# Second block of a two-block transformer: the meta tokens' value products as one product over 80 zero-padded rows

## The chip, the cores and the metric

The kernel runs on one core of a Trainium2 chip. The metric is the device time of one execution in microseconds (us). Of the kernel before, three runs are shown; their median is 2448.92 us (2448.57 to 2449.99).

## What is computed

Two transformer blocks follow each other on 512 tokens of width 1024, all in float32. The first block is a stick-breaking attention layer and a sparse attention layer, each with a squared-ReLU MLP. The change lies in the second block, which puts 16 meta tokens beside the 512 tokens and runs two attentions over all 528:

```python
u = rms_norm_2(h, g_mix)                       # h: meta tokens and the first block's output, 528 x 1024
qa, ka, va, qb, kb, vb, ga, gb = split(u @ w_in)
# diff_attention, 8 heads, two maps m per head, values 128 wide
p = softmax(q_m k_m^T / sqrt(64) - slope * dist)
w = p[0] - lam * p[1]
oa = rms_norm_2(w @ va, g_subln) * 0.8
# gqa_attention, 8 query heads, 2 key/value heads of 128
ob = softmax(axial_rope(qh) axial_rope(kh)^T / sqrt(128)) @ vb
merged = sigmoid(ga) * (oa @ w_branch_a) + sigmoid(gb) * (ob @ w_branch_b)
h = h + merged @ w_out
h = h + expert_choice_ffn(rms_norm_2(h, g_ffn))   # 16 experts, 66 tokens each
```

## The kernel before

Every float32 operand of a matrix product is kept in two float32r parts, h (the value rounded) and l (the rest), and a product x·w is made of three: h·h, l·h and h·l. Weights stream in as units of 128 x 1024: `unit` (L169) issues the load on SP's queue, ScalarE makes w_h (L185) and GpSimd or VectorE makes w_l (L186). `proj2` (L797) multiplies a unit with all 528 tokens in two halves of 264 columns; its products have the line L208.

The token axis is cut into five tiles, `TT`: four of 128 tokens and, last, the 16 meta tokens. Keys are taken in these five tiles, queries in two halves, `QH`: tiles 0 and 1 (256 queries), then tiles 2, 3 and the meta tile (272 queries).

Values: `vproj2` (L836) takes, for each token tile, 24 products (three kinds times 8 slices of 128 inputs) with the tile's columns of uh or ul as the stationary operand and 256 columns of the weights moving; the meta tile has a stationary operand of 16 columns. ScalarE writes the h part of the result, scaled by the token's factor rt, and VectorE the l part (L846, L847). `vproj2u` (L813) does the same for the first pair of heads, with all five tiles in three PSUM banks, so that the products don't wait for rt (L824, L830, L831). There are five such projections: four pairs of heads of the differential attention, and one for the grouped-query attention.

Attention: per head and query tile, the scores go into PSUM (L998 to L1003, and L1133), VectorE and ScalarE make the softmax (L1004 to L1012, L1135 to L1139), and the weights stay as row tiles e (queries on the partitions, 528 keys along). `av2` (L849) turns them and multiplies them with the values. For each key tile k it transposes each query tile's block on TensorE (L862), with as many rows and columns as the tiles have; ScalarE copies the result as h part pt_h (L866), VectorE makes pt_l (L867), and three products vh·pt_h, vl·pt_h and vh·pt_l are summed in the bank `av` (L871). For the meta tile of keys these three have a contraction of 16 rows. For the meta tile of queries the transposes have 16 rows:

```python
nc.tensor.transpose(pt[0:kn, c:c + qn], w[t][0:qn, ko:ko + kn], self.ident[0:qn, 0:qn])
```

So `av2` runs 32 times (8 heads, two halves, two attentions), with 25 transposes per head, five of them from the meta tile of queries.

A scheduler puts the instructions of all engines in an order, from the order in the code, the operands and the pools' buffers; each engine then runs its own list in that order. While a head's softmax runs, TensorE's list holds projections of later heads. The pools that the change touches: e0 (6 buffers of 128 x 528), e1 (3), v (2), the PSUM pools `tr` (2 banks), `av` (1), `mm` and `sc`. After the two attentions follow the gates and output projections (`merge`) and the experts, whose weights are most of the data that the kernel reads.

Of the kernel before, what the change touches and what calls it, by code (L numbers as in the profile page):

```python
# [7 lines left out]
F32 = mybir.dt.float32  # L8
F32R = mybir.dt.float32r
# [12 lines left out]
def ounits(w, groups):  # L22
    """Output weights by group of head pairs, in units of some columns for all pairs of the group."""
# [114 lines left out]
class Kern:  # L138
# [83 lines left out]
    def square(self, kt, eng=None, pool=False):  # L222
        """acc += x^2"""
# [20 lines left out]
    def rs(self, eps, rt, rr, pp=None):  # L244
        """rt[128, 4]: 1/rms by token on the partitions; rr[128, 512]: the same along the free axis."""
# [49 lines left out]
    def vproj(self, xh, xl, src):  # L295
        """x times two weight units; the four token tiles lie in two banks, each with one start for both of its tiles."""
# [27 lines left out]
    def av_causal(self, P, off, v, po, first, last):  # L324
        """po += v.T @ P.T for a causal P kept as row tiles at the offsets off."""
# [110 lines left out]
    def oproj(self, src, groups, todo, os_, after):  # L436
        """Output projection of the units todo of (group, unit), added to the residual."""
# [33 lines left out]
    def rope_sum(self, src, f, pool, pp, on_pool=0):  # L471
        """src * cos + rot(src) * sin, where f has the two parts of src."""
# [56 lines left out]
    def cmp_in(self, kp, c, xs, pos):  # L529
        """The compression blocks with their positions added, by block position pair and block, in two parts."""  # L530
# [12 lines left out]
    def cmp_raws(self, kp, k0):  # L543
        """Compression weights from unit k0 on, loaded ahead into the place of tiles that are done with."""
# [268 lines left out]
    def vproj2u(self, src, rt, v):  # L813
        """vproj2 with all token tiles at once, two in a bank, so that the products need no wait for rt"""
# [3 lines left out]
        for u in range(2):  # L818
            w = self.unit(src[u])
            for t, (o, n) in enumerate(self.TT):  # L820
                p = ps[t // 2][0:n, t % 2 * 256:t % 2 * 256 + 256]
                for a, (x, wi) in enumerate(((self.uh, 0), (self.ul, 0), (self.uh, 1))):
                    for k in range(4):
                        nc.tensor.matmul(p, x[:, u * 4 + k, o:o + n], w[wi][:, k * 256:k * 256 + 256],  # L824
                                         start=u == 0 and t % 2 == 0 and a == 0 and k == 0,
                                         stop=u == 1 and (t % 2 == 1 or t == 4) and a == 2 and k == 3)
        for t, (o, n) in enumerate(self.TT):
            p = ps[t // 2][0:n, t % 2 * 256:t % 2 * 256 + 256]
            r = rt[0:n, t:t + 1]
            nc.scalar.activation(v[0:n, t, 0], p, AF.Copy, scale=r)  # L830
            nc.vector.scalar_tensor_tensor(v[0:n, t, 1], p, r, v[0:n, t, 0].bitcast(F32), op0=OP.mult, op1=OP.subtract)  # L831
# [4 lines left out]
    def vproj2(self, src, rt, v):  # L836
        nc = self.nc
        wv = [self.unit(src[i]) for i in range(2)]
        for t, (o, n) in enumerate(self.TT):
            ps = self.mm.tile([128, 512], F32, name="mm")[0:n, :256]  # L840
# [801 lines left out]
```

## Time and profile before

| | before |
|---|---|
| median of three runs | 2448.92 us |
| the profiled execution: span from its first instruction to its last | 2447.4 us |
| TensorE products busy | 2357.8 us, 96% |
| VectorE busy | 1561.4 us, 64% |
| ScalarE busy | 1264.1 us, 52% |
| GpSimd busy | 677.3 us, 28% |
| share of the chain that ended last, by engine | PE 55%, DVE 6%, issue 4%, DMA 3%, POOL 2%, ACT 2% |

For the profiled execution the span is the only time on record; its time by the clock of the runs isn't shown, so the span is set against the median: 1.5 us less.

How to read it: PE is TensorE's products, PEld its loads of stationary operands, DVE VectorE, ACT ScalarE, POOL GpSimd. Where a form such as 16*128 stands with a product, it is the stationary operand: 16 rows (the contraction) by 128 columns (the rows of the result). A group's mean is the length of one instruction from its start to its modelled end; products overlap, so the steps between starts, not these lengths, add up to the stretch.

### The profile page before, as it was taken

What the parts mean: (1) busy time and instruction counts of PE and PEld (TensorE: products, weight loads), DVE (VectorE), ACT (ScalarE), POOL (GpSimd) and SP (SyncE); (2) the same over time, 40 slices, a digit from 0 to 9 for tenths busy, and PEclk for the clock granted to TensorE, in tenths of its full rate; (3) what the DMA queues carried; (4) which work ended last, traced back from release to release, by engine and by line L of the source; (5) the groups of instructions that cost most, each with busy time, mean ns of one, the idle gap of its engine ahead of it and who ended that gap; (6) DMA issues with size and microseconds to landing.
All of it is one profiled execution on the core that took longest, in us unless ns stands there. A gap on an engine that the chain in (4) does not pass through costs nothing.

```text
span 2447.4 us, 36010 instructions
## 1 busy us (share of the span) xinstructions
PE 2357.8 (96%) x13626; PEld 1946.2 (80%) x13626; DVE 1561.4 (64%) x2754; ACT 1264.1 (52%) x2269; POOL 677.3 (28%) x573
## 2 busy tenths in 40 slices
PE   8999999999989999899999999999999999699997
PEld 7887788888877777688888899889899999566664
DVE  6887543444586878643443677867666654588996
ACT  6665423223355767523223456555465533378885
POOL 0000322223325444222222632333454311111100
PEclk9999999999999999999999999999999999899998
DMA  4222223222432111122222321222211144689994
GB/s 143 78 78 87 69 95 95 95 95 95 132 120 77 36 37 43 52 95 95 94 90 93 123 79 53 70 60 63 70 44 44 44 174 155 229 302 370 375 390 144
DMA packets 85806, 286.57 MB, mean 117 GB/s; under 512 B 12197, under 2 KB 14117, under 8 KB 85633
## 3 DMA queue, kind: packets, MB, share of 16 engines
q1 hardware_dynamic: 79008, 273.78, 33.4%
q0 software_dynamic: 3360, 8.12, 1.6%
q10 hardware_dynamic: 3264, 2.38, 0.4%
q8 instruction: 107, 1.75, 0.3%
q14 instruction: 67, 0.54, 0.1%
HBM read 257.05 MB, written 12.37 MB: 110 GB/s over the span
## 4 chain that ended last, share of the span: by engine, by line
PE 55%; DVE 6%; issue 4%; DMA 3%; POOL 2%; ACT 2%; POOLq 0%; DVEq 0%; SPq 0%; ACTq 0%
PE mm L208 28%; PE mm L1495 5%; PE av L871 3%; PE mm L843 2%; PE mm L1517 2%; PE tr L862 2%; PE av L346 2%; PE mm L1048 1%; PE sc L1133 1%; PE mm L450 1%; PE tr L336 1%; PE sc L998 1%; PE sc L741 1%; PE sc L1003 1%; DMA res<-in_e_gate_dram 1%
## 5 line engine op out<-in xcount | busy, mean ns | idle before, releaser
L185 ACT CAST w_h<-w_raw 128x1024 fp32r<-128x1024 f32 x269 | 281.3, 1046 | 374.5 <-PE mm L208 285.9
L186 DVE TENSOR_TENSOR w_l<-w_raw,w_h 128x1024 fp32r<-128x1024 f32 x209 | 316.4, 1514 | 235.1 <-ACT w_h L185 234.4
L208 PE MATMUL mm<-uh,w_h 128*128 128x512 f32 (+1 forms) x1440 | 315.2, 352 | 14.6 <-ACT w_h L185 8.7
L208 PE MATMUL mm<-uh,w_l 128*128 128x512 f32 (+1 forms) x1440 | 309.0, 348 | 0.0
L208 PE MATMUL mm<-ul,w_h 128*128 128x512 f32 (+1 forms) x1440 | 306.1, 346 | 0.0
L208 PEld LDWEIGHTS mm<-uh,w_h 128*128 128x128 f32 x1440 | 238.5, 191 | 53.7 <-ACT w_h L185 9.0
L208 PEld LDWEIGHTS mm<-uh,w_l 128*128 128x128 f32 x1440 | 237.3, 190 | 35.9 <-issue 0.6
L208 PEld LDWEIGHTS mm<-ul,w_h 128*128 128x128 f32 x1440 | 234.9, 188 | 34.2
L186 POOL TENSOR_TENSOR w_l<-w_raw,w_h 128x1024 fp32r<-128x1024 f32 x60 | 144.8, 2417 | 158.2 <-ACT w_h L185 156.5
L782 POOL TENSOR_TENSOR relu<-relu 128x512 f32<-128x512 f32 x64 | 98.4, 1537 | 271.9 <-ACT hh L781 265.5
L780 ACT ACTIVATE relu<-mm 128x512 f32<-128x512 f32 x64 | 38.3, 598 | 232.6 <-PE mm L208 232.6
L788 POOL TENSOR_TENSOR res<-res,mt 128x512 f32<-128x512 f32 x62 | 90.4, 1459 | 214.1 <-DVE mt L787 214.1
L787 DVE TENSOR_TENSOR mt<-mm,rs 128x512 f32<-128x512 f32 x64 | 44.1, 690 | 139.0 <-PE mm L208 139.0
L208 PE MATMUL mm<-hh,w_h 128*128 128x512 f32 x512 | 131.4, 397 | 0.0
L208 PE MATMUL mm<-hh,w_l 128*128 128x512 f32 x512 | 130.7, 395 | 0.0
L208 PE MATMUL mm<-hl,w_h 128*128 128x512 f32 x512 | 130.7, 395 | 0.0
L235 POOL TENSOR_TENSOR acc<-acc,sq 128x512 f32<-128x512 f32 x28 | 42.5, 1519 | 304.9 <-ACT sq L233 304.6
L1495 PE MATMUL mm<-ul,xe 128*66 128x512 f32 x412 | 119.2, 397 | 0.1
L208 PEld LDWEIGHTS mm<-hh,w_h 128*128 128x128 f32 x512 | 95.9, 189 | 25.2 <-ACT w_h L185 3.4
L208 PEld LDWEIGHTS mm<-hh,w_l 128*128 128x128 f32 x512 | 96.6, 189 | 22.4
L208 PEld LDWEIGHTS mm<-hl,w_h 128*128 128x128 f32 x512 | 96.6, 189 | 22.4
L186 DVE TENSOR_TENSOR ol<-w_raw,ul 128x1024 fp32r<-128x1024 f32 x86 | 103.3, 1221 | 15.2 <-ACT ul L185 11.6
(525 smaller groups left out, 5439.6 us busy)
## 6 DMA issues: line engine op xcount, KB each, us to landing
w_raw<-in_w_dram SPq DMA_DIRECT2D x128, 512.0 KB, 3.5
w_raw<-in_e_down_dram SPq DMA_DIRECT2D x37, 512.0 KB, 11.1
w_raw<-in_e_gate_dram SPq DMA_DIRECT2D x34, 512.0 KB, 10.6
w_raw<-in_e_up_dram SPq DMA_DIRECT2D x34, 512.0 KB, 12.1
raws<-in_e_gate_dram SPq DMA_DIRECT2D x20, 512.0 KB, 11.0
raws<-in_e_up_dram SPq DMA_DIRECT2D x20, 512.0 KB, 11.4
raws<-in_e_down_dram SPq DMA_DIRECT2D x19, 512.0 KB, 11.7
res<-in_e_gate_dram SPq DMA_DIRECT2D x10, 512.0 KB, 10.6
```

Source lines behind the costliest of these rows:

```text
L185: nc.scalar.copy(h, raw)
L186: (nc.gpsimd if self.we else nc.vector).tensor_tensor(l, raw, h.bitcast(F32), op=OP.subtract)
L208: nc.tensor.matmul(ps, w[:, k * 128:(k + 1) * 128], x[k], start=start and a == 0 and k == 0, stop=stop and a == 2 and k == nk - 1)
L346: nc.tensor.matmul(po[:, j * 128:512], v[j], src[:, c:c + w], start=first and j == 0 and s == 0, stop=last and gi == 2 and s == 1)
L782: nc.gpsimd.tensor_tensor(r, r, r, op=OP.mult)
L787: nc.vector.tensor_tensor(t, ps, r2, op=OP.mult)
L788: (nc.vector if c == 3 and m == 7 else nc.gpsimd).tensor_tensor(res[:, m, 0:512], res[:, m, 0:512], t, op=OP.add)
L843: nc.tensor.matmul(ps, x[:, k, o:o + n], wv[k // 4][wi][:, (k % 4) * 256:(k % 4 + 1) * 256], start=a == 0 and k == 0, stop=a == 2 and k == 7)
L862: nc.tensor.transpose(pt[0:kn, c:c + qn], w[t][0:qn, ko:ko + kn], self.ident[0:qn, 0:qn])
L871: nc.tensor.matmul(po, x(k), y[0:kn, c], start=k == 0 and a == 0, stop=k == 4 and a == 2)
L1495: nc.tensor.matmul(ps, x[:, 2 * i + k], w[:, k * 512:k * 512 + 512], start=i == 0 and a == 0 and k == 0, stop=i == 3 and a == 2 and k == 1)
L1517: self.pe_last = nc.tensor.matmul(py[j], x[:, k], w[:, j * 512:j * 512 + 512], start=k == 0 and a == 0, stop=k == 3 and a == 2)
```

## The change

In the second block alone:

- The values of the meta tile go into a tile of their own, v4 (96 x 256, zeroed once): h part in rows 0 to 15, l part in rows 32 to 47, h part again in rows 64 to 79. The turned weights of the meta keys go into p4 (zeroed, two of them in turn): h part in rows 0 to 15 and 32 to 47, l part in rows 64 to 79. One product over rows 0 to 79 then sums the three (`av2`).
- The weights of the meta queries are kept in e4 (128 x 528, two in turn, zeroed), of which only the first 16 rows are written; every transpose takes 128 rows and the whole identity, so those of the meta queries have 128 moving columns in place of 16.
- In the V projections the meta tile's columns of uh and ul lie side by side in um (128 x 8 x 48, zeroed, uh in columns 0 to 15, ul in 32 to 47). One product with w_h gives both, in rows 0 to 15 and 32 to 47 of PSUM; `vkeep` adds the two with a copy on ScalarE and an addition on VectorE. 16 products per projection take the place of 24.
- The pool e0 has 5 buffers in place of 6, the value tiles 4 token tiles in place of 5; the zeroing is done by GpSimd.

The rest of the diff is comments, and `rank` and others are unchanged. Its core:

```diff
-    def vproj2u(self, src, rt, v):
+    def vproj2u(self, src, rt, v, v4):
...
+    def vmul(self, p, w, u, t, start, stop):
+        nc = self.nc
+        o, n = self.TT[t]
+        xs = ((self.uh, 0), (self.ul, 0), (self.uh, 1)) if t < 4 else ((self.um, 0), (self.uh, 1))[::1 - 2 * u]
+        for a, (x, wi) in enumerate(xs):
+            for k in range(4):
+                y = x[:, u * 4 + k] if x is self.um else x[:, u * 4 + k, o:o + n]
+                nc.tensor.matmul(p[0:y.shape[-1]], y, w[wi][:, k * 256:k * 256 + 256], start=start and a == 0 and k == 0,
+                                 stop=stop and a == len(xs) - 1 and k == 3)
+
+    def vkeep(self, p, rt, v, v4, t):
+        nc = self.nc
+        r = rt[0:self.TT[t][1], t:t + 1]
+        if t < 4:
+            h, l = v[:, t, 0], v[:, t, 1]
+        else:
+            h, l = v4[0:16], v4[32:48]
+            m = self.tp.tile([128, 512], F32, name="sq", bufs=2)[0:16, 0:256]
+            nc.scalar.copy(m, p[32:48])
+            nc.vector.tensor_tensor(m, p[0:16], m, op=OP.add)
+            p = m
+            nc.scalar.activation(v4[64:80], p, AF.Copy, scale=r)
+        nc.scalar.activation(h, p, AF.Copy, scale=r)
+        nc.vector.scalar_tensor_tensor(l, p, r, h.bitcast(F32), op0=OP.mult, op1=OP.subtract)
...
+    def meta_tiles(self, at):
+        nc = self.nc
+        e, p = ([at.tile([128, n], F32 if a == "e4" else F32R, name=f"{a}{i}") for i in range(2)] for a, n in (("e4", 528), ("p4", 272)))
+        for x in e + p:
+            nc.gpsimd.memset(x if x.dtype == F32 else x.bitcast(F32), 0.0)
+        self.e4, self.p4 = itertools.cycle(e), itertools.cycle(p)
...
-            kn = self.TT[g[0]][1]
             for j, k in enumerate(g):
-                ko = self.TT[k][0]
+                ko, kn = self.TT[k]
                 for t in tiles:
-                    qo, qn = self.TT[t]
-                    c = j * on + qo - o0
-                    nc.tensor.transpose(pt[0:kn, c:c + qn], w[t][0:qn, ko:ko + kn], self.ident[0:qn, 0:qn])
+                    c = j * on + self.TT[t][0] - o0
+                    nc.tensor.transpose(pt[0:kn, c:c + 128], w[t][:, ko:ko + kn], self.ident)
             n = len(g) * on
+            if g[0] == 4:
+                h = next(self.p4)[:, :n]
+                for o in (0, 32):
+                    nc.scalar.copy(h[o:o + 16], pt[0:16, :n])
+                nc.vector.tensor_tensor(h[64:80], pt[0:16, :n], h[0:16].bitcast(F32), op=OP.subtract)
+                nc.tensor.matmul(po, v4[0:80], h[0:80], start=False, stop=True)
+                continue
...
+                    full = at.tile([128, 528], F32, name="e0", bufs=5) if t < 4 else next(self.e4)
...
+                    self.vb4 = kp.tile([96, 256], F32R, name="vb4")
+                    nc.gpsimd.memset(self.vb4.bitcast(F32), 0.0)
+                    self.um = kp.tile([128, 8, 48], F32R, name="um")
+                    nc.gpsimd.memset(self.um.bitcast(F32), 0.0)
+                    nc.scalar.copy(self.um[:, :, 0:16], self.uh[:, :, 512:528].bitcast(F32))
+                    nc.scalar.copy(self.um[:, :, 32:48], self.ul[:, :, 512:528].bitcast(F32))
```

The scheduler makes new lists from this. TensorE's list in the grouped-query attention, in the first half of a head's queries. vb is the tile of values, e a tile of softmax weights, k and q keys and queries; a row's shape is that of the result. Before:

```order
L1133 MATMUL sc<-k_16006,q 128x264 x6
L208 MATMUL mm<-ul,w_h 128x264 x4
L871 MATMUL av<-pt_h,vb 128x256 x2
L208 MATMUL mm<-ul,w_h 128x264 x2
L871 MATMUL av<-pt_l,vb 128x256
L862 MATMUL tr<-ident,e_16504 128x128
L862 MATMUL tr<-ident,e_16530 128x16
L862 MATMUL tr<-ident,e_16517 128x128
L862 MATMUL tr<-ident,e_16530 128x16
```

With the change, at the same place:

```order
L1169 MATMUL sc<-k_15948,q 128x264 x6
L208 MATMUL mm<-ul,w_h 128x264 x7
L208 MATMUL mm<-uh,w_h 128x264 x3
L884 MATMUL tr<-ident,e_16274 128x128
L891 MATMUL av<-p_16276,vb_11546 128x256
L884 MATMUL tr<-ident,e_16451 128x128
L884 MATMUL tr<-ident,e_16464 128x128
L884 MATMUL tr<-ident,e_16274 128x128
```

The three L871 rows over the 16 meta keys (two from pt_h, one from pt_l, with projections in between) have become the one L891, which stands 10 rather than 4 projection products behind the scores; the meta queries' transposes (e_16530, now e_16274) write 128 columns in place of 16.

TensorE's list where the last V projection (of the grouped-query attention) ends. um is the tile with both parts of the meta tokens' x. Before:

```order
L843 MATMUL mm<-w_l,uh 128x256 x8
L881 MATMUL tr<-sq,ones 128x272
L843 MATMUL mm<-w_h,uh 16x256 x8
L843 MATMUL mm<-w_h,ul 16x256 x8
L843 MATMUL mm<-w_l,uh 16x256 x8
```

With the change:

```order
L834 MATMUL mm<-w_l,uh 128x256 x4
L891 MATMUL av<-p_11578,v_11584 128x272
L834 MATMUL mm<-w_h,um 48x256 x4
L834 MATMUL mm<-w_l,uh 16x256 x8
L834 MATMUL mm<-w_h,um 48x256 x4
```

24 products for the meta tile have become 16, eight of them with a stationary operand of 48 columns.

GpSimd's list where the differential attention starts. w_l is the l part of a weight unit; acc is the sum of squares of the first block's output. Before:

```order
L186 TENSOR_TENSOR w_l<-w_raw,w_h 128x1024
L235 TENSOR_TENSOR acc<-acc,sq 128x512
L186 TENSOR_TENSOR w_l<-w_raw,w_h 128x1024 x5
L1011 TENSOR_SCALAR e_11867<-e_11867,st,lam 128x528
```

With the change:

```order
L235 TENSOR_TENSOR acc<-acc,sq 128x512
L870 MEMSET e_11575 128x528
L870 MEMSET e_11576 128x528
L870 MEMSET p_11577 128x272
L870 MEMSET p_11578 128x272
L993 MEMSET v_11583 96x256
L993 MEMSET v_11584 96x256
L186 TENSOR_TENSOR w_l<-w_raw,w_h 128x1024 x5
```

Six fills stand ahead of the third weight unit's l part; the first two units and acc are ahead of them, as before.

## Rows read from the trace of the kernel before

**Rows 1.** Busy time by stretch: differential attention, grouped-query attention, experts.

```profile
core 0: us, PE busy (x) PEld busy (x) DVE busy (x) ACT busy (x) POOL busy (x), PEclk, DMA share, GB/s
1425.00:1725.00 300.00, 295.76 (x2278) 273.90 (x2277) 224.98 (x690) 173.97 (x397) 92.42 (x65) 1.00 0.20 59
1765.00:1960.00 195.00, 195.00 (x1489) 178.98 (x1488) 123.66 (x319) 117.37 (x271) 85.14 (x77) 1.00 0.14 44
2143.00:2400.00 257.00, 256.93 (x1232) 156.52 (x1232) 227.78 (x235) 213.68 (x260) 35.34 (x24) 0.99 0.98 357
```

**Rows 2.** What PE waited for, 1425 to 1725 us (total, times, longest).

```profile
PE av L871 <- DVE pt_l L867: 2.0, 1, 2.0
```

**Rows 3.** Timeline of PEld, first meta-key products (start, length, then the form).

```profile
1446.09 0.66 PEld L843 LDWEIGHTS mm<-w_h,uh 128*128 128x128 f32 x5
1446.89 0.29 PEld L871 LDWEIGHTS av<-pt_h,v 16*128 16x128 f32 x2
1447.32 0.30 PEld L843 LDWEIGHTS mm<-w_h,uh 128*128 128x128 f32 x2
...
1447.77 0.31 PEld L843 LDWEIGHTS mm<-w_h,ul 128*128 128x128 f32 x2
1448.21 0.18 PEld L871 LDWEIGHTS av<-pt_l,v 16*128 16x128 f32 x1
1448.53 0.20 PEld L862 LDWEIGHTS tr<-ident,e 128*128 128x128 f32 x2
```

**Rows 4.** Timeline of PEld, one of the last meta-key products.

```profile
1961.16 0.91 PEld L208 LDWEIGHTS mm<-uh,w_h 128*128 128x128 f32 x7
1962.21 0.29 PEld L871 LDWEIGHTS av<-pt_h,vb 16*128 16x128 f32 x2
1962.63 0.19 PEld L208 LDWEIGHTS mm<-uh,w_h 128*128 128x128 f32 x1
```

**Rows 5.** Timeline of PEld, a transpose of the meta queries.

```profile
1456.63 0.26 PEld L862 LDWEIGHTS tr<-ident,e 128*128 128x128 f32 x2
1457.05 0.14 PEld L862 LDWEIGHTS tr<-ident,e 16*128 16x128 f32 x1 [0.17 <-issue]
1457.22 0.19 PEld L998 LDWEIGHTS sc<-ks,qd 128*128 128x128 f32 x1
```

**Rows 6.** PE's groups by form (count | busy us, mean ns | idle before).

```profile
L862 PE MATMUL tr<-ident,e 16*128 16x16 f32 x64 | 13.0, 225 | 0.0
L871 PE MATMUL av<-pt_h,v 16*128 16x272 f32 x16 | 4.1, 336 | 0.0
L871 PE MATMUL av<-pt_l,v 16*128 16x272 f32 x8 | 3.1, 386 | 0.0
L862 PE MATMUL tr<-ident,e 16*16 16x16 f32 x16 | 2.9, 178 | 0.0
```

**Rows 7.** Timeline of PEld, a stationary operand of 16 columns behind one of 128.

```profile
1538.22 0.19 PEld L1003 LDWEIGHTS sc<-ks,qd 128*128 128x128 f32 x1
1538.33 0.10 PEld L998 LDWEIGHTS sc<-ks,qd 128*16 128x16 f32 x1
```

**Rows 8.** Timeline of PEld in the experts: a transpose over 66 rows.

```profile
2163.41 0.37 PEld L1495 LDWEIGHTS mm<-ul,xe 128*66 128x66 f32 x2
2163.88 0.14 PEld L1482 LDWEIGHTS tr<-ident,ya 66*128 66x128 f32 x1
2164.11 0.20 PEld L1495 LDWEIGHTS mm<-ol,xe 128*66 128x66 f32 x2
```

**Rows 9.** What DVE waited for, 1425 to 1725 us.

```profile
DVE st L1008 <- ACT e L1007: 17.8, 31, 1.8
DVE e L1004 <- PE sc L1003: 17.0, 24, 3.2
```

**Rows 10.** Groups by form of ACT, DVE and POOL, 1400 to 1980 us.

```profile
L866 ACT CAST pt_h<-tr 16x272 fp32r<-16x272 f32 x16 | 5.9, 370 | 12.4 <-PE tr L862 12.4
L867 DVE TENSOR_TENSOR pt_l<-tr,pt_h 16x272 fp32r<-16x272 f32 x16 | 6.8, 426 | 10.1 <-ACT pt_h L866 10.0
L1011 POOL TENSOR_SCALAR e<-e,st,lam 128x528 f32<-128x528 f32 x32 | 25.7, 804 | 100.9 <-DVE st L1008 85.0 <-DVE st L1006 8.5 <-PE tr L862 3.8
```

**Rows 11.** Timelines where the differential attention starts: POOL, then ACT.

```profile
1389.52 1.28 POOL L235 TENSOR_TENSOR acc<-acc,sq 128x512 f32<-128x512 f32 x1 [1.97 <-ACT sq L233]
1398.27 2.39 POOL L186 TENSOR_TENSOR w_l<-w_raw,w_h 128x1024 fp32r<-128x1024 f32 x1 [7.47 <-ACT w_h L185]
...
1389.90 0.28 ACT L908 CAST uh<-mt 128x128 fp32r<-128x128 f32 x1
1391.59 0.31 ACT L911 ACTIVATE mt<-res 128x128 f32<-128x128 f32 x1 [1.41 <-DVE ul L909]
```

More of the change, by code (lines that the diff above doesn't have):

```diff
@@ L819, in vproj2u @@
             w = self.unit(src[u])
[L820 to L831, printed above, removed]
+            for t in range(5):
+                self.vmul(ps[t // 2][:, t % 2 * 256:t % 2 * 256 + 256], w, u, t, u == 0 and t % 2 == 0, u == 1 and (t % 2 == 1 or t == 4))
@@ new lines, in vproj2u @@
+        for t in range(5):
+            self.vkeep(ps[t // 2][:, t % 2 * 256:t % 2 * 256 + 256], rt, v, v4, t)
+    def vmul(self, p, w, u, t, start, stop):
[7 more added lines that the diff above has]
+                                 stop=stop and a == len(xs) - 1 and k == 3)
@@ L833 @@
     VB = ("mm", "tr", "tr")
     VH = (0,)
-    def vproj2(self, src, rt, v):
-        nc = self.nc
-        wv = [self.unit(src[i]) for i in range(2)]
-        for t, (o, n) in enumerate(self.TT):
-            ps = self.mm.tile([128, 512], F32, name="mm")[0:n, :256]
-            for a, (x, wi) in enumerate(((self.uh, 0), (self.ul, 0), (self.uh, 1))):
-                for k in range(8):
-                    nc.tensor.matmul(ps, x[:, k, o:o + n], wv[k // 4][wi][:, (k % 4) * 256:(k % 4 + 1) * 256],
-                                     start=a == 0 and k == 0, stop=a == 2 and k == 7)
-            r = rt[0:n, t:t + 1]
-            nc.scalar.activation(v[0:n, t, 0], ps, AF.Copy, scale=r)
-            nc.vector.scalar_tensor_tensor(v[0:n, t, 1], ps, r, v[0:n, t, 0].bitcast(F32), op0=OP.mult, op1=OP.subtract)
@@ L849, in av2, with vproj2 @@
-    def av2(self, at, w, half, vh, vl):
+    def vproj2(self, src, rt, v, v4):
+        wv = [self.unit(src[i]) for i in range(2)]
+        for t in range(5):
+            ps = self.mm.tile([128, 512], F32, name="mm")[:, :256]
+            for u in range(2):
+                self.vmul(ps, wv[u], u, t, u == 0, u == 1)
+            self.vkeep(ps, rt, v, v4, t)
+    def meta_tiles(self, at):
+        nc = self.nc
+        e, p = ([at.tile([128, n], F32 if a == "e4" else F32R, name=f"{a}{i}") for i in range(2)] for a, n in (("e4", 528), ("p4", 272)))
+        for x in e + p:
+            nc.gpsimd.memset(x if x.dtype == F32 else x.bitcast(F32), 0.0)
+        self.e4, self.p4 = itertools.cycle(e), itertools.cycle(p)
@@ L851, in av2 @@
+    def av2(self, at, w, half, vh, vl, v4):
         nc = self.nc
@@ L870, in av2 @@
                 for a, (x, y) in enumerate(((vh, h), (vl, h), (vh, l))):
-                    nc.tensor.matmul(po, x(k), y[0:kn, c], start=k == 0 and a == 0, stop=k == 4 and a == 2)
+                    nc.tensor.matmul(po, x(k), y[:, c], start=k == 0 and a == 0, stop=False)
         return po
@@ L960, in diff_attention @@
         os_, late = [], []
+        self.meta_tiles(at)
+        v4s = [at.tile([96, 256], F32R, name=f"v4{i}") for i in range(2)]
+        for x in v4s:
+            nc.gpsimd.memset(x.bitcast(F32), 0.0)
         for head in range(8):
             if head % 2 == 0:
[L963 to L964 removed]
+                v = at.tile([128, 4, 2, 256], F32R, name="v", bufs=2)
+                v4 = v4s[head // 2 % 2]
+                (self.vproj2u if head in self.VH else self.vproj2)(I["a_v"][head:head + 2], self.rt, v, v4)
             sl = at.tile([128, 128], F32R, name="sl", bufs=2)
```

26 lines of the change are left out of this document (13 added, 13 removed).

## The prediction

> **What bounds the kernel now.** I read the busy time by stretch first. In the differential attention TensorE is busy 295.76 of 300 us, in the grouped-query attention all of 195 [rows 1]; VectorE, the next, has 75% and 63%. TensorE's own list of waits in the first stretch has as its longest entry one of 2.0 us, a product behind pt_l [rows 2]. So in both attentions time is the sum of TensorE's steps, and what shortens a step shortens the run, until another engine takes over. Behind them the experts run 257 us with the DMA engines at 98% [rows 1]; their loads start when buffers of the attentions and of the merge come free, so they move up with the attentions.
>
> Then I looked at what a step costs, in the timeline of the loads of stationary operands (PEld). Loads come one per product. Five of them with 128 rows stretch over 0.66 us [rows 3]; one is 0.19 long [rows 4], so the step is (0.66 − 0.19)/4 = 0.12 us. Where the 16-row products of the meta keys come in, it is longer. The last of those five starts at 1446.09 + 0.66 − 0.19 = 1446.56; two 16-row loads follow at 1446.89 and the next 128-row load at 1447.32 [rows 3]. That is 0.76 us for three steps, which should take 0.36: **0.40 us too much**. The single 16-row load behind it shows the same: from 1447.89 (1447.77 + 0.31 − 0.19) to 1448.53 is 0.64 for two steps, 0.40 too much. Near the end of the grouped-query attention it is 0.75 for three steps, 0.39 too much [rows 4]. So the engine pays for going to 16 rows and for coming back, about 0.2 us each way, whatever the number of products between.
>
> **What the change removes.**
>
> *Meta-key products.* `av2` runs 32 times. Each time two 16-row products from pt_h and one from pt_l become one: 64 products of 0.12 us, 7.7 us. In the trace the pair and the single product lie apart, with projections between [rows 3], so each run of `av2` pays two visits: 64 × 0.40 = 25.6 us, if 80 rows cost no visit. Together 33.3 us.
>
> *Transposes of the meta queries.* 64 with a 16*128 operand and 16 with 16*16 [rows 6]. A single one: the 128-row transposes ahead of it start last at 1456.63 + 0.26 − 0.14 = 1456.75, and the load behind it comes at 1457.22 [rows 5]: 0.47 us for two steps, 0.23 too much. With 128 rows and 128 columns it costs one common step, as its neighbours do (0.26 − 0.14 = 0.12 us from one to the next, [rows 5]). Some of the 80 stand side by side and share a visit. Always alone gives 80 × 0.23 = 18.4 us, always in pairs 9.2 us; I take 60 visits, 13.8 us, since the list of TensorE puts 128-row transposes between most of them.
>
> *V projections.* Five, each with 24 − 16 = 8 products fewer: 40 × 0.12 = 4.8 us. The stationary operand grows from 16 to 48 columns. A load of 16 columns behind one of 128 comes 0.11 us later [rows 7], no more than a common step, so a narrow operand costs no visit today, and I take none for 48 columns. The Trainium skill speaks against this: TensorEngine Tiling (Array Packing), section Key Properties, says that a change of tiling mode drains the engine, and lists 32, 64 and 128 columns as different modes. By that, 48 and 16 columns side by side would need a change in each of the ten units, and at 0.4 us each the sum would be 4 us smaller; the row above shows no such drain for columns.
>
> The sum of what TensorE is spared: 33.3 + 13.8 + 4.8 = **51.9 us**, of which some 28 in the differential attention (half of the first two, all of the third) and 24 in the other.
>
> **What it adds.**
>
> *80 rows instead of 16.* The trace of before has no product with 80 rows. The nearest is a transpose with 66 in the experts: the loads around it stand at 2163.64 (2163.41 + 0.37 − 0.14), 2163.88 and 2164.11, the pace of the 512-column products next to it (2163.41 to 2163.64), and the second load behind it follows after 0.20 − 0.14 = 0.06 us, the short step of a 66-column transpose [rows 8]. So it costs no visit. Ends: nothing, or 32 × 0.40 = 12.8 us as with 16 rows. I take nothing, as 80 is nearer to 66.
>
> *ScalarE.* One more copy into p4 per run of `av2`, 32 × 0.37 = 11.8 us; two more operations per V projection at about the same price, 3.7 us. They lie beside TensorE's products, since ScalarE is busy 174 of 300 and 117 of 195 us [rows 1, 10]. The chain from the transposes to the meta product grows by the copy, 0.37 + 0.37 + 0.43 in place of 0.37 + 0.43 for the l part; the scheduler's new list has ten projection products ahead of it where four stood, 1.2 us. If that cover is missing, the chain is the stall of the rival below.
>
> *VectorE.* Five additions of about 0.43 us: 2 us in 495.
>
> *GpSimd.* Fills: six at the start of the differential attention, four at that of the other, two earlier. None is in the trace; from below nothing, from above a tensor-scalar operation over 128 x 528, 0.80 us [rows 10], though four of the six are half as wide. Six are under 4.8 us and stand where GpSimd now waits 7.47 us for the next unit's h part [rows 11]. I take nothing. Without that gap the third unit's l part would come later, and the projection behind it.
>
> *The opening.* The first copy into um stands between L908 and L911 on ScalarE, the second behind L911, about 0.28 us each [rows 11]; the sums of squares for rt wait for L911. Also, the first copy lets the meta products of the first V projection start later. I take 1 us, ends 0 and 2.
>
> *New waits.* With 28 us less, VectorE's 225 us would fill 83% of 272. It already waits for ScalarE and for the scores, 17.8 and 17.0 us [rows 9], so it isn't evenly loaded, and in places it will hold TensorE. Ends: nothing, or half of the gain there, 14 us. I take 5 us, nearer the first, because TensorE today waits for it almost never [rows 2].
>
> **The forecast.** 51.9 − 1 − 5 = 46 us. Against the profiled span, 2447.4 − 46 = 2401.4 us; the median of the runs is 1.5 us higher, 2448.9 − 46 = **2403 us**.
>
> **The rivals.**
>
> 1. *VectorE becomes the bound in the differential attention.* For: its share, and ScalarE's chain through it. Against: the grouped-query attention, with 63%, has no such limit. The gain there is halved and the forecast's 5 us become 14: 2412 us; with waits in the other attention as well, 2418. 12%.
> 2. *80 rows pay a visit as 16 did.* Against: the 66 rows. 32 × 0.40 = 12.8 us back: 2416 us. 6%.
> 3. *The loads of the experts don't move up*, because their start is set by something that doesn't depend on the attentions. For: 98% of DMA time there [rows 1]. Against: in the grouped-query attention the DMA engines are at 14%, so the loads aren't running ahead; they wait for buffers. 2449 us. 4%.
> 4. *Slower: the one meta product becomes a stall.* It starts only when p4 is whole, and TensorE runs its list in order, so all projections behind it wait too. The point from which this decides is 52/32 = 1.6 us per run of `av2`. The one wait for pt_l in the trace was 2.0 us [rows 2]; if each of the 32 took that, 64 us would be lost against 46 gained by the rest: 2467 us. Against: that stretch shows it once, before a product over 128 rows. 3%.
>
> **How the numbers follow.** The forecast has 73%; 2% is left for what I don't see. The forecast's own range is 2392 (all 51.9 us, and all transposes alone, 4.6 more) to 2411 (transposes in pairs and 3 us more of waits). To hold 8 in 10 with rivals 1 and 2, and both together in part, it reaches to 2425. About 0.2%, 5 us, is what a measurement of this kernel can tell from no change. Faster by more than that: forecast and rivals 1 and 2, with most of what I don't see, 92%. Within 0.2%: rival 3 and a little, 4%. Slower: rival 4 and a little, 4%.
>
> **What would show it.** In the profile after: the 80-row loads at a step of 0.12 us from their neighbours, and the L862 forms with 16 rows gone; 64 + 40 products fewer on TensorE; the stretch of both attentions shorter by 28 and 24 us less the waits; the experts' stretch as long as before. It is wrong if the gap around the 80-row loads is 0.3 or more, if TensorE's waits in the attentions grow by over 15 us, if the fills on GpSimd delay a unit's l part, or if the experts' stretch grows by what the attentions lose.

## The result, and the profile after

The changed kernel takes 2416.3 us (median of four runs, 2415.7 to 2418.3), the kernel before 2448.9 us in the same session (2448.6 to 2450.0). The ratio is 0.9869, with a 95% interval of 0.9856 to 0.9881: 32.6 us faster, where 46 were forecast. The profiled execution is the longest of the four, 2418.27 us with a span of 2416.2; the other three have spans of 2413.7 to 2414.3.

| | before | after |
|---|---|---|
| TensorE products busy | 2357.8 us, x13626 | 2319.7 us, x13522 |
| VectorE busy | 1561.4 us | 1560.2 us |
| ScalarE busy | 1264.1 us | 1277.2 us |
| GpSimd busy | 677.3 us | 679.1 us |

The 104 products are gone, ScalarE has 13 us more. The windows answer to [rows 1], the last two starting 10 and 30 us earlier than there:

```profile
core 0: us, PE busy (x) PEld busy (x) DVE busy (x) ACT busy (x) POOL busy (x), PEclk, DMA share, GB/s
1425.00:1715.00 290.00, 275.22 (x2199) 264.44 (x2199) 223.08 (x688) 179.26 (x415) 92.70 (x65) 0.99 0.20 61
1755.00:1935.00 180.00, 180.00 (x1498) 177.04 (x1496) 120.49 (x319) 120.15 (x285) 84.79 (x77) 1.00 0.15 51
2113.00:2370.00 257.00, 256.93 (x1239) 156.61 (x1238) 228.00 (x235) 213.65 (x260) 35.31 (x24) 0.99 0.99 358
```

The grouped-query attention is still nothing but TensorE's steps, and the experts are as long as before. In the differential attention TensorE now stands still for 15 of 290 us, where it was 4 of 300. What it waits for there (total, times, longest) answers to [rows 2]:

```profile
PE sc L1033 <- DVE e L1039: 5.0, 6, 1.9
PE tr L884 <- DVE e L1047: 4.5, 4, 2.4
PE mm L208 <- DVE rs L1008: 1.4, 1, 1.4
PE av L891 <- DVE p L890: 1.2, 1, 1.2
```

L1039 and L1047 are the softmax on VectorE (L1004 and L1012 before). The loads of stationary operands (PEld; start, length, form) show the new products, to be set against [rows 3, 5, 7]:

```profile
1448.48 0.19 PEld L834 LDWEIGHTS mm<-w_l,uh 128*128 128x128 f32 x1
1448.61 0.19 PEld L891 LDWEIGHTS av<-p,v 80*128 80x128 f32 x1
1448.74 0.25 PEld L884 LDWEIGHTS tr<-ident,e 128*128 128x128 f32 x2
...
1449.33 0.31 PEld L834 LDWEIGHTS mm<-w_l,uh 128*128 128x128 f32 x2
1449.56 0.12 PEld L834 LDWEIGHTS mm<-w_h,um 128*48 128x48 f32 x1
1449.68 0.26 PEld L884 LDWEIGHTS tr<-ident,e 128*128 128x128 f32 x2
...
1457.41 0.19 PEld L900 LDWEIGHTS av<-pt_l,v 128*128 128x128 f32 x1
1457.55 0.31 PEld L884 LDWEIGHTS tr<-ident,e 128*16 128x16 f32 x3
1457.87 0.19 PEld L208 LDWEIGHTS mm<-uh,w_l 128*128 128x128 f32 x1
```

A load over 80 rows stands 0.13 us behind its neighbour and the next one 0.13 behind it; one with 48 columns is followed by the next after 0.12 us; three transposes of the meta keys' weights, the third of them from the meta queries, take 0.32 us together. None pays the 0.40 or 0.23 us of before. PE's groups by form (count | busy, mean ns | idle before) answer to [rows 6]; the forms with a stationary operand of 16 rows are gone from both attentions:

```profile
L884 PE MATMUL tr<-ident,e 128*16 128x128 f32 x80 | 14.9, 272 | 0.0
L834 PE MATMUL mm<-w_h,um 128*48 128x256 f32 x32 | 6.5, 285 | 0.0
L891 PE MATMUL av<-p,v 80*128 80x272 f32 x8 | 2.6, 322 | 0.0
L891 PE MATMUL av<-p,vb 80*128 80x272 f32 x8 | 2.5, 316 | 1.2 <-DVE p L890 1.2
```

**Where the time went.** I followed the starts of all loads from one landmark to the next, and split each stretch into common steps (0.118 us each), what the steps beside a 16-row operand have over that (visits), and what other steps have over it where it is more than 0.25 us (gaps).

| stretch | before | after | less |
|---|---|---|---|
| first V product to the first score product of the differential attention | 42.7 | 41.1 | 1.6 |
| from there to the first grouped-query score (loads / visits / gaps) | 344.5 (2589 / 20.3 / 10.5) | 336.1 (2525 / 0 / 28.2) | 8.4 |
| from there to the last product with the values | 204.9 (1551 / 19.4 / 0.6) | 185.7 (1526 / 0 / 2.6) | 19.2 |
| merge and experts, to the end | 475.1 | 473.4 | 1.7 |

In the differential attention 64 loads fewer are 7.6 us and the visits 20.3: 27.9 us spared, the 28 of the forecast. Of these the gaps took 17.7 back and smaller delays 1.8, so that 8.4 arrived. That row is where most of the missing 13 us are, and the experiments ask what the gaps are. The grouped-query attention gave 19.2 us where 24 were forecast: its gaps grew by 2.0, and it lost 25 loads, not 32, between these landmarks. The opening and the stretch behind the attentions gave 3.3 us that weren't forecast.

One gap of the differential attention can be followed through four engines, in the order of time (start, length, then the instruction, in brackets the idle time before it):

```profile
1470.11 2.38 POOL L186 TENSOR_TENSOR w_l<-w_raw,w_h 128x1024 fp32r<-128x1024 f32 x1 [1.99 <-ACT w_h L185]
1470.27 2.23 DVE L1041 TENSOR_TENSOR st<-st 16x1 f32<-16x1 f32 x1
1472.59 0.74 ACT L1042 ACTIVATE e<-e,st 16x528 f32<-16x528 f32 x1 [1.31 <-DVE st L1041]
1473.71 1.07 POOL L1046 TENSOR_SCALAR e<-e,st,lam 16x528 f32<-16x528 f32 x1 [1.23 <-DVE st L1043]
1475.44 0.76 DVE L1047 SCALAR_TENSOR_TENSOR e<-e,st,e 16x528 f32<-16x528 f32 x1
1476.26 0.69 PE L884 MATMUL tr<-ident,e 128*128 128x128 f32 x2 [2.44 <-DVE e L1047]
```

L1041, the minimum of the two halves' minima, has one element per row. It took 2.23 us and ended at 1472.50, just when GpSimd's product of two SBUF operands ended (1470.11 + 2.38 = 1472.49). ScalarE's exponential waits for it, GpSimd and VectorE behind that (L1047 starts 0.66 us after GpSimd's result is there, behind another VectorE instruction), and at the end TensorE for 2.44 us. The Trainium skill (SBUF — State Buffer, section Who interferes with whom) says that VectorE with two SBUF inputs and GpSimd reading SBUF exclude each other for a whole instruction; the rows agree. All 80 of these minima (shortest, median and longest in ns), in the changed kernel

```profile
L1041 DVE TENSOR_TENSOR st<-st x80: 127/153/2359, 1425.1 to 1698.8; 128x1 f32<-128x1 f32 x64, 16x1 f32<-16x1 f32 x16
```

and in the kernel before:

```profile
L1006 DVE TENSOR_TENSOR st<-st x80: 126/153/2309, 1427.0 to 1703.8; 128x1 f32<-128x1 f32 x64, 16x1 f32<-16x1 f32 x16
```

So they were blocked before as well, and by more: all 80 together took 19.7 us more than 80 times their shortest before, and 16.2 us with the change. Whether that cost anything there is a question for the runs.

The minima are not the only instructions of VectorE that are held up. The last step of the softmax, L1047, also has two tensor operands in SBUF; in the changed kernel all 40 of them, and one that TensorE's transposes waited for directly, were:

```profile
L1047 DVE SCALAR_TENSOR_TENSOR e<-e,st,e x40: 736/763/2862, 1428.4 to 1701.0; 128x528 f32<-128x528 f32 x32, 16x528 f32<-16x528 f32 x8
```

```profile
1502.74 2.39 POOL L186 TENSOR_TENSOR w_l<-w_raw,w_h 128x1024 fp32r<-128x1024 f32 x1
1503.06 2.64 DVE L1047 SCALAR_TENSOR_TENSOR e<-e,st,e 128x528 f32<-128x528 f32 x1
1505.76 0.88 PE L884 MATMUL tr<-ident,e 128*128 128x128 f32 x6 [0.84 <-DVE e L1047]
```

Adding up over all of VectorE's instructions in the differential attention what each took beyond the shortest of its line and form gives 64 us before and 61 us with the change. So VectorE was held up no longer in all than before, while TensorE's gaps grew.

### The profile page after: what moved, and what is told of

Its sections match the earlier page's. It is cut to its first block, busy times and chain, and to the rows that moved or that the text cites. A ratio compares the mean times of both kernels' runs of the same rounds, so it can differ in the third digit from the quotient of the medians.

```text
span 2416.2 us, 35835 instructions
## 1 busy us (share of the span) xinstructions
PE 2319.7 (96%) x13522; PEld 1933.5 (80%) x13522; DVE 1560.2 (65%) x2759; ACT 1277.2 (53%) x2313; POOL 679.1 (28%) x585
## 3 DMA queue, kind: packets, MB, share of 16 engines
q10 hardware_dynamic: 3264, 2.38, 0.4%
## 4 chain that ended last, share of the span: by engine, by line
PE 49%; DVE 9%; issue 6%; ACT 3%; POOL 2%; DMA 2%; POOLq 0%; ACTq 0%; DVEq 0%; SPq 0%
PE mm L208 25%; PE mm L1538 6%; PE mm L1560 3%; PE av L346 2%; PE av L900 1%; PE tr L884 1%; PE mm L450 1%; PE sc L1169 1%; PE tr L336 1%; PE mm L834 1%; DVE e L1039 1%; DVE e L1047 1%; PE sc L741 1%; PE mm L1083 1%; ACT w_h L185 1%
## 5 line engine op out<-in xcount | busy, mean ns | idle before, releaser
L186 DVE TENSOR_TENSOR w_l<-w_raw,w_h 128x1024 fp32r<-128x1024 f32 x209 | 315.5, 1510 | 236.3 <-ACT w_h L185 235.6
L208 PE MATMUL mm<-uh,w_h 128*128 128x512 f32 (+1 forms) x1440 | 310.2, 352 | 15.0 <-ACT w_h L185 8.8
L186 POOL TENSOR_TENSOR w_l<-w_raw,w_h 128x1024 fp32r<-128x1024 f32 x60 | 145.8, 2432 | 145.3 <-ACT w_h L185 145.2
L186 DVE TENSOR_TENSOR ol<-w_raw,ul 128x1024 fp32r<-128x1024 f32 x86 | 103.2, 1220 | 12.2 <-ACT ul L185 11.7
```

Of the source, the lines that this page charges most:

```text
L186: (nc.gpsimd if self.we else nc.vector).tensor_tensor(l, raw, h.bitcast(F32), op=OP.subtract)
L208: nc.tensor.matmul(ps, w[:, k * 128:(k + 1) * 128], x[k], start=start and a == 0 and k == 0, stop=stop and a == 2 and k == nk - 1)
```

## The experiments

Times are medians of four runs or more; the ratio to the kernel before has its 95% interval. Theory in all of them: TensorE's steps became cheaper by what was forecast, and in the differential attention waits for the softmax on VectorE took part of it back. The rivals are named in each expectation. The table at the end of this section holds the gaps of all kernels, each from its one profiled run, which lies up to 3.4 us from the median; where an expectation speaks of gaps of 5 us before and 20 in the change, they are counted only to the last V product, and by the table's landmarks 10.5 and 28.2.

**The 80-row product alone.** From the change, back to 16-row transposes, the pool e0 of before and 24 V products (which still go through one weight unit and then the other, as in the change; no run tests that order by itself):

```diff
-                    nc.tensor.transpose(pt[0:kn, c:c + 128], w[t][:, ko:ko + kn], self.ident)
+                    nc.tensor.transpose(pt[0:kn, c:c + qn], w[t][0:qn, ko:ko + kn], self.ident[0:qn, 0:qn])
...
-        xs = ((self.uh, 0), (self.ul, 0), (self.uh, 1)) if t < 4 else ((self.um, 0), (self.uh, 1))[::1 - 2 * u]
+        xs = ((self.uh, 0), (self.ul, 0), (self.uh, 1))
```

> The kernel before with the 80-row product alone: values in v4, turned weights in p4; the transposes of the meta queries keep 16 rows and 16 columns, the V projections keep 24 products for the meta tile. Theory A (each visit to 16 rows costs TensorE 0.40 us, and what is not gained in the differential attention goes into new waits there for VectorE and its softmax chain): TensorE is spared 33.3 us, some 9 us come back as waits, about 2425 us, and the loads around the 80-row operand show no gap. Rival B (80 rows pay a visit as well): 12.8 us more, about 2438 us, with gaps of 0.3 us or more around the 80-row loads.

2428.2 us, ratio 0.9919 (0.9902 to 0.9935): 20 us of the 33.3 that the sum had for it, 3 us above theory A and 10 below rival B. Its trace shows where 4.6 of the missing 13 are: the visits of both attentions fell from 39.8 to 18.8 us, by 21.0 and not by 25.6, since the 65 visits that the transposes of the meta queries still pay cost 0.29 us each there and 0.22 in the kernel before.

**The transposes over 128 rows alone**, on the kernel before, with e4 and the smaller pool e0:

```diff
-                    nc.tensor.transpose(pt[0:kn, c:c + qn], w[t][0:qn, ko:ko + kn], self.ident[0:qn, 0:qn])
+                    nc.tensor.transpose(pt[0:kn, c:c + 128], w[t][:, ko:ko + kn], self.ident)
```

> The kernel before with the transposes alone over 128 rows (e4 tiles, whole identity); products and V projections as before. Theory A: 54 to 60 visits of 0.2 us go, 11 to 14 us, some 3 us come back as waits, about 2438 us. Rival B (moving 128 columns in place of 16 costs as much as the visit): 2445 to 2449 us.

2434.4 us, ratio 0.9941 (0.9924 to 0.9957): 14 us, the sum's 13.8. The two parts alone give 34, and the whole change 32.6, so nothing is left for the third part if the parts add up.

**The V projections undone**, the rest as in the change (the second hunk of the first experiment, and `vkeep` without its copy and addition for the meta tile):

> The changed kernel with the V projections put back to 24 products for the meta tile (um left out); the 80-row product and the transposes stay. Theory A: 40 products of 0.12 us come back to TensorE, but 32 of them in the differential attention, where it now waits for VectorE, so at most half is seen: 2417 to 2419 us. Rival C (TensorE still sets the time there, and what is missing has to do with the order of the lists): the full 4.8 us, 2421 us or more. The rival that the um part costs something itself: below 2416 us.

2414.0 us, ratio 0.9861 (0.9844 to 0.9877): not slower by the 4.8 us of the sum, if anything 2 faster, and the intervals overlap. The part gives nothing in time. Its products do cost their steps: the differential attention has 32 loads more than in the change, 3.8 us, but gaps of 18.8 us in place of 28.2.

**A lighter softmax.** In the changed kernel the shift of the softmax of the differential attention becomes the maximum over one half of the keys; the other half's accumulators and the minimum of both are left out:

```diff
-                            nc.vector.tensor_scalar(x[:, s], ps, -1.0, None, op0=OP.mult, op1=OP.min,
-                                                    accum_out=st[0:n, 2 + j:3 + j])
-                        nc.vector.tensor_tensor(st[0:n, 0:1], st[0:n, 2:3], st[0:n, 3:4], op=OP.min)
+                            if j == int(t in (2, 3)):
+                                nc.vector.tensor_scalar(x[:, s], ps, -1.0, None, op0=OP.mult, op1=OP.min, accum_out=st[0:n, 0:1])
+                            else:
+                                nc.vector.tensor_scalar(x[:, s], ps, -1.0, None, op0=OP.mult)
```

> The changed kernel with less work for VectorE in the differential attention: the shift of the softmax is the maximum over one half of the keys (that with the query's own tile) and not over both, so 80 of the 160 reads of the accumulator (0.08 us) and the 80 minimum operations (0.33 us for 128 rows) go, some 30 of 223 us; the softmax is the same but for the shift. Theory A: the waits for score banks and softmax weights in the differential attention, 17 us above those of before, fall by more than half, about 2405 us. Rival C (the waits come from the scheduler's order or the longer chain through p4): they stay, 2413 to 2417 us.

2405.1 us, ratio 0.9821 (0.9805 to 0.9838): 11 us come back, theory A's number, as if the waits hung on VectorE's part of the softmax. Whether on its load, on the blocked minima, which this edit also removes, or on the lists, which the scheduler made anew (some 1300 of TensorE's 13522 instructions run at another place), it does not tell.

**Another tile for m**, since `vkeep` takes m from the two buffers in which the head normalisation puts its squares:

```diff
-            m = self.tp.tile([128, 512], F32, name="sq", bufs=2)[0:16, 0:256]
+            m = self.lm[0:16].rearrange("p a b -> p (a b)")
```

> The changed kernel with one edit: the sum of the meta tile's two parts in the V projections (m) goes into a tile of its own life (lm) in place of one of the two buffers sq. Theory S (the V part costs because m takes an sq buffer from the head normalisation, whose inv_rms chain then starts later, and TensorE waits): the loss of the V part goes, 2411 to 2414 us. Theory R (the V part only gives another order of the lists, and what waits in the differential attention is the softmax chain through VectorE, as the run with the lighter softmax showed): the same as the change, 2416, give or take 2, and the differential attention again about 295 us from first to last score product. Theory C (the longer chain copy, addition, copy, copy itself delays the values of the meta keys): the same time, with waits of the 80-row products on v4.

2410.0 us, ratio 0.9842 (0.9825 to 0.9858): 1 us below theory S's range and far from theory R's. But the scheduler also put some 1200 of TensorE's 13522 instructions elsewhere, so by itself this run can't part buffer and order.

**Two lines swapped.**

```diff
-            nc.scalar.activation(v4[64:80], p, AF.Copy, scale=r)
         nc.scalar.activation(h, p, AF.Copy, scale=r)
         nc.vector.scalar_tensor_tensor(l, p, r, h.bitcast(F32), op0=OP.mult, op1=OP.subtract)
+        if t == 4:
+            nc.scalar.activation(v4[64:80], p, AF.Copy, scale=r)
```

> The changed kernel with two lines in another order: for the meta tile the copy of the h part into rows 64 to 79 is written behind the l part in place of ahead of it. No instruction is added or taken away, no buffer changes. Theory R (the order that the scheduler makes decides how much of the gain the waits take): the time moves by 2 us or more in either direction, by the sum of the TensorE gaps over 0.25 us in the differential attention. Otherwise: 2416 within 1.5 us, gaps of about 20 us there as in the change.

2419.5 us, ratio 0.988 (0.9863 to 0.9896), 3 us up with overlapping intervals. Only 5 of TensorE's 13522 instructions run at another place, so it says little either way.

**The lighter softmax on the kernel before** (the same edit):

> The kernel before with the lighter softmax of the differential attention: the shift is the maximum over one half of the keys in place of the maximum over all, so 80 accumulator reads and 80 small minima go from VectorE. Theory W (before the change TensorE's own steps set the pace in the differential attention; VectorE became a limit only when the change shortened them): little or nothing, 2444 to 2448 us, gaps over 0.25 us falling from 5 to 2 at the most. Rival (the softmax chain already cost as much before): as in the changed kernel, about 11 us less, 2437.

2444.3 us, ratio 0.9982 (0.9972 to 0.9991): 4.4 us, against 11 in the changed kernel. It is just inside theory W's range: taking this work away gains less before.

**The lighter softmax with the V projections undone** (both edits):

> The changed kernel with both: the lighter softmax (maximum over one half of the keys) and the V projections of before, three products per slice for the meta tile. With the lighter VectorE the V part has no reason to cost in waits. Theory D (the V part's 40 products are worth 0.12 us each where nothing waits): 4 to 5 us slower than the lighter softmax alone, 2409 to 2410 us. Theory N (the V part gives nothing even there, since its products over 16 columns were already cheaper or its chain costs what they save): 2403 to 2406. Theory S (it costs through the buffer or the chain whatever VectorE's load): 2402 to 2403.

2405.5 us, ratio 0.9823 (0.9807 to 0.9839), like the lighter softmax alone: theory N. Its 40 products less are worth nothing there too: the 32 loads in the differential attention are again 3.8 us, and the gaps there are 12.7 us in place of 16.4, so what the part spares in steps it loses in gaps. Whether TensorE would have waited in those places anyway was not tried.

**The minimum with one tensor operand**, the rest as in the change:

```diff
-                        nc.vector.tensor_tensor(st[0:n, 0:1], st[0:n, 2:3], st[0:n, 3:4], op=OP.min)
+                        nc.vector.tensor_scalar(st[0:n, 0:1], st[0:n, 2:3], st[0:n, 3:4], None, op0=OP.min)
```

> The changed kernel with one operation in another form: the minimum of the two halves' minima (80 on VectorE, 0.13 to 0.15 us each, up to 2.4 us where GpSimd is in a product of two SBUF operands) takes its second value as a scalar operand in place of a second tensor. The computation and the count of instructions stay. In the differential attention of the changed kernel these 80 took some 15 us more than 80 times their shortest; by the Trainium skill (SBUF, State Buffer; section Who interferes with whom) a VectorE instruction with two SBUF inputs is blocked while GpSimd reads SBUF, and one with a single SBUF input is not. Theory P (what TensorE waited for in the differential attention was the softmax chain, held up in these minima by GpSimd): none over 0.5 us any more, and 2406 to 2411 us, most of what the lighter softmax gave. Theory L (it was VectorE's load as such, 225 of 290 us): the blocked time goes to the next instruction with two inputs or changes nothing, 2414 to 2418.

2403.3 us (2402.2 to 2403.6), ratio 0.9815 (0.9799 to 0.9832): 13 us below the change, more than theory P had. The 80 minima, the window of the differential attention and the first two entries of TensorE's waits in that kernel:

```profile
L1041 DVE TENSOR_SCALAR st<-st x80: 182/206/218, 1421.3 to 1684.4; 128x1 f32<-128x1 f32 x64, 16x1 f32<-16x1 f32 x16
```

```profile
1425.00:1715.00 290.00, 282.21 (x2266) 272.88 (x2265) 221.95 (x691) 188.30 (x432) 100.37 (x71) 0.99 0.21 65
```

```profile
PE mm L208 <- DVE st L1043: 2.0, 1, 2.0
PE tr L884 <- DVE e L1047: 2.0, 3, 1.1
```

Each is some 50 ns longer at its shortest, and none is over 0.22 us. VectorE is as busy as in the change (221.95 against 223.08 of 290 us), so its load as such wasn't the bound; TensorE's busy time rose by 7 us in a window of the same length. Two things keep this from being the price of the blocked minima alone: some 1200 of TensorE's instructions run at another place here too, and L1047 is still held up, to 2.93 us at the longest.

**The own tile with the lines swapped**, another order with the same buffers:

> The changed kernel with the own tile for m and with the two lines of the meta tile's values in the other order. Against the run with the own tile alone some 420 rows of TensorE's list stand elsewhere; against the change, 765. Theory S (sharing sq cost the 6 us): 2410 give or take 2 again, in another order of the lists. Theory R (the own tile gave a lucky order): anywhere from 2410 to 2419, most likely near 2416.

2411.4 us, ratio 0.9847 (0.9831 to 0.9863): as theory S had it.

**The own tile and the minimum with one tensor operand together:**

> The changed kernel with both: the own tile for m and the minimum with one tensor operand. If the two are separate causes, the gains add up: 2400 to 2405 us. If both only remove the same waits of TensorE in the differential attention (some 20 us of long gaps there in the change, 14 with the own tile), the sum is smaller: 2405 to 2410. If both were only other orders of the lists: 2410 or more.

2409.0 us, ratio 0.9841 (0.9824 to 0.9857): the gains don't add up. The time lies where both edits would remove the same waits, but that doesn't explain why it is above that of the minimum alone. The own tile now costs 5.7 us against the run with the minimum alone, where by itself it had gained 6.3; so it has no price of its own that could be carried over, and theory S falls in spite of the two runs that came within 1 us of its numbers. The minimum's form gains 1 us beside the own tile, within the spread of the runs, and 13 without. What both edits share is that each moves over a thousand of TensorE's instructions; from the minimum alone to both it is some 1400.

**The minimum with one tensor operand in the kernel before:**

> The kernel before with the minimum of the two halves' minima in the form with one tensor operand, as in the run that took the change from 2416 to 2403. Theory X (before, the minima were blocked as long as after, 18.7 us beyond their shortest, but beside TensorE's own steps, so that the change only laid the wait open): 2443 to 2448 us, a third of the 13 us or less. Rival (the blocked minima cost the kernel before as much; then the form of the minimum has nothing to do with where the change's gain went): 2434 to 2438 us.

2442.1 us, ratio 0.9973 (0.9963 to 0.9983): 6.2 us, 1 us below theory X's range and 4 above the rival's: between both theories. Here too the lists changed, by some 540 of TensorE's instructions.

Together, by landmarks of the loads (the differential attention from its first score product to the first grouped-query score, in us):

| kernel | median | stretch | visits | gaps |
|---|---|---|---|---|
| before | 2448.2 to 2448.9 | 344.5 | 20.3 | 10.5 |
| before, lighter softmax | 2444.3 | 341.3 | 19.3 | 6.9 |
| before, minimum with one operand | 2442.1 | 339.5 | 20.1 | 6.3 |
| product alone | 2428.2 | 337.0 | 10.7 | 14.5 |
| transposes alone | 2434.4 | 338.2 | 12.7 | 12.4 |
| change | 2416.3 | 336.1 | 0 | 28.2 |
| change, lines swapped | 2419.5 | 339.4 | 0 | 30.1 |
| change, V undone | 2414.0 | 330.8 | 0 | 18.8 |
| change, own tile | 2410.0 | 329.0 | 0 | 21.5 |
| change, own tile, swapped | 2411.4 | 331.1 | 0 | 24.0 |
| change, own tile, minimum | 2409.0 | 327.1 | 0 | 18.9 |
| change, lighter softmax | 2405.1 | 325.1 | 0 | 16.4 |
| change, lighter, V undone | 2405.5 | 323.0 | 0 | 12.7 |
| change, minimum with one operand | 2403.3 | 324.9 | 0 | 15.8 |

Nine kernels have the 80-row product and the wide transposes. The five with blocked minima have gaps of 18.8 to 30.1 us and a mean time of 2414.2; the four without have 12.7 to 18.9 and 2405.7. That is 8.5 us in the mean over several orders, though two of the four also have the lighter softmax. Kernels with the same work and the same buffers or nearly so lie apart by as much: 2410.0 to 2419.5 for the change with or without own tile and swap, 2403.3 and 2409.0 with the other minimum. The change as it was made has one of the two slowest orders of its group. Among the five with blocked minima the amount of blocking doesn't set the gaps: beyond 80 times their shortest the minima took 16.2 us in the change, 16.8 with the lines swapped, 23.6 with the own tile, 24.2 with the own tile swapped and 24.2 with the V part undone, and the gaps are 28.2, 30.1, 21.5, 24.0 and 18.8: larger where less was blocked. That leaves the places at which TensorE's list meets a late instruction, which no run shows by itself.

## Why the prediction was right, and where it was off

The side and the range were right (2392 to 2425 held 2416.3), the likeliest time was 13 us too low. The time lies above 2411, where the forecast's own range ended; it was held by the part that had been added for rivals 1 and 2, of which the rows exclude one and bear out the other only in place. So the range was right in part by luck. By its steps:

- *What is spared.* Right. The visits were put at 25.6 + 13.8 = 39.4 us; the loads of before show 20.3 in the differential attention and 19.4 in the other, 39.8. The differential attention was spared 27.9 us, as forecast. The pieces alone agree for the transposes (14 us measured, 13.8 forecast) and not for the product (20 for 33.3): it spared 21.0 us of visits in place of 25.6, and in the differential attention gaps rose from 10.5 to 14.5.
- *80 rows and 48 columns pay nothing.* Right: steps of 0.13 and 0.12 us. The Trainium skill's rule that a change of tiling mode drains the engine (TensorEngine Tiling (Array Packing), section Key Properties) agrees with the loads of before for 16 rows, about 0.2 us each way; for 16 and 48 columns the loads show no such drain. Rival 2, with almost the time that came out (2416), is excluded by them.
- *V projections, 4.8 us.* Wrong: nothing, in two settings (2416.3 and 2414.0; 2405.1 and 2405.5). The steps are spared, 3.8 us of them in the differential attention, but gaps take as much or more.
- *ScalarE's copies.* In the differential attention hidden but for one wait of 1.2 us behind the subtraction. At the end of the grouped-query attention the cover was gone, which the sum had no term for: few projections are left there, and the chain of copies and subtraction lies open, 1.39 us ahead of the last meta product, with 0.44 for the l part of an earlier key tile, in PEld's timeline:

```profile
1940.54 0.19 PEld L900 LDWEIGHTS av<-pt_l,vb 128*128 128x128 f32 x1 [0.44 <-DVE pt_l L896]
...
1942.83 0.19 PEld L891 LDWEIGHTS av<-p,vb 80*128 80x128 f32 x1 [1.39 <-DVE p L890]
```

- *GpSimd's fills and the opening.* The fills cost nothing: the third unit's l part starts at 1397.29 us, not later than before (1398.27), with 4.79 us of idle time still ahead of it. The opening became 1.6 us shorter where 1 longer was forecast.
- *New waits, 5 us (0 to 14).* This is the term that failed: gaps grew from 10.5 to 28.2 us, 17.7 us, beyond the upper end. The reason given, that TensorE "waits for it almost never", looked at TensorE's waits before and not at what was late behind them: instructions of VectorE stood there at up to 2.3 us (the minima) and 2.9 us (L1012, now L1047), and TensorE hardly waited for them. With the minima freed on both sides, the change takes 2442.1 to 2403.3, 38.8 us in place of 32.6, and gaps go from 6.3 to 15.8, so some 9 us of new waits remain even then. How much of the difference is the freed minima and how much the other lists isn't shown.
- *Rival 1.* Its place was right, the differential attention, and its times (2412 and 2418) lie about the result. Its mechanism wasn't: VectorE isn't full (77% of the window), and the run with the other minimum has it as busy with 13 us less. The waits that could be followed come from single instructions that are late; in all VectorE was held up no longer than before (61 us against 64).
- *Rivals 3 and 4.* The last product with the values comes 29.5 us earlier, and the experts behind it are as long as before; waits for the 80-row product's weights are there, but of 1.2 us once in the differential attention and once at the end of the other, not 2.0 at each of 32.

What remains open: why the V part's gain goes into gaps, and which property of an order of the lists makes its gaps; no run held the order fixed while a buffer or a form changed. A rival for the rest of the waits stands untested: that they come from the other instructions with two tensor operands, L1047 first, whose form no run changed.

## To carry to other kernels

Counting what an engine's steps cost more than the common step gave what the whole edit spares on that engine to within a microsecond, though not what each piece spares alone; how much of it arrives depends on what is late behind the steps, so look for instructions of the next engine that are far longer than their shortest, also where nobody waits for them yet. Where a scheduler makes the lists, one run of an edit may be one draw: here kernels that differ only in a buffer for m and in the place of one line lay up to 9.5 us apart, so try an edit in two or three surroundings before giving it a price. And where GpSimd works beside it, try a small VectorE operation with one tensor operand and a scalar operand in place of two tensors; here that was faster in two of three settings, by 13 and 6 us, and no different in the third.

## What the runs showed of the hardware that was not expected

An operation on one element per row took up to 2.36 us on VectorE in place of 0.13. Of the 80 in the changed kernel 12 took over 0.5 us, and each of these ended within 0.02 us of the end of a GpSimd instruction, eight with the product L186 and four with L1046. The same value computed with a scalar operand took 0.18 to 0.22 us in all 80 cases. No other line was changed for that, though the scheduler's lists were; the kernel became 13 us faster with the change and 6.2 before it; beside the own tile it was 1 us, within the spread of the runs.
